# Gates ahead of the attention, squares on GpSimd, and four output tiles begun with four heads, in a Griffin-style decoder layer

## The chip, the cores and the metric

The kernel runs on one core of one Trainium2 chip. The metric is the device time of one execution in microseconds (us); lower is better. Engines are TensorE (PE in the profile; PEld are its weight loads), VectorE (DVE), ScalarE (ACT), GpSimd (POOL) and SyncE (SP), which issues most of the DMAs.

## The reference

One decoder layer on 1024 tokens with 1024 channels, in float32. What matters here is branch A with its gates:

```python
proj = h @ w_in                      # q, k, v, pool input, memory q, gate logits (3 x 1024 columns)
a = diff_attention(q_d, k_d, v_d, lam)        # 8 heads, two softmax maps each, causal, ALiBi
a = rms_norm(a, subln_g) * (1.0 - lam_init)   # per head, over its 128 channels
y_attn = a.reshape(B, S, 1024) @ w_attn_branch
gates = sigmoid(gate_logits).reshape(B, S, 3, 1024)
mix = gates[:, :, 0] * y_attn + gates[:, :, 1] * y_pool + gates[:, :, 2] * y_mem
x = x + rms_norm(mix @ w_out)
```

A gated feed-forward part with a convolution over tokens follows, which the change does not touch.

## The kernel before

**Products.** Every float32 operand is split into a rounded part and the rest (`split`, L87: ScalarE rounds, L89, VectorE subtracts, L90), and a product is three matmuls (`mm3`, L102: high by high, high by low, low by high). Two tiles of 128 output channels over all tokens are either computed directly (`gate`, L1112: 48 matmuls of 128x512 a tile, 96 for two) or together as seven products of half blocks with sums of blocks (`seven`, L198, called by `channels`: 7 x 12 = 84 matmuls for the pair; its weight pages are split just before they are used). Keys' tile pair, the four pairs of queries and gates 0 and 1 go through `seven` ahead of the attention.

**Attention.** Eight heads run in turn, four query blocks of 256 tokens each. A block's stages are `scores` (L1161 on TensorE; L1165 on VectorE adds the bias and takes the maximum, L1170 on ScalarE is the exponential), `combine` (the two maps together, L1181 to L1184 on VectorE), `turn_weights` (transposes, L1200, then a split into aT), `weigh_values` (L1217, the products with the values into poa) and `head_norm` (L1235, the sum of the squares, sq, over the head's channels by two matmuls with ones into pn, stored to ss_d). The squares' high part is rounded on ScalarE (L1225), the low part subtracted on VectorE (L1226). Each block's result goes to DRAM (ao_d). `weave` (L257) puts fillers between the stages: next head's keys, values and queries, and steps of `gate`. The table GATES sets that gate tiles 2 and 3 fill head 0 and tile 4 fills head 7.

**After it.** Gates 5 to 7 run between the last head and the first output product. `load_norms` and `head_norms` turn the sums of four heads into reciprocal norms (hn, small VectorE operations L1260 to L1266) and store them (r_d, L1267); each head is loaded again (a, L1381) with its norm spread over the partitions (rb, L1383), scaled (L1384, VectorE) and split into ath (ScalarE) and atl (VectorE). `merge_heads` (L1356) multiplies heads by the output weights of the branch into pya; output tiles 0 and 1 are begun with heads 0 to 3 while heads 4 to 7 are still on their way. `merge` (L1403) multiplies by the gate and adds the other branches.

**Order.** Each engine runs its instructions in the order of its queue; a scheduler derives it from the code, pools and dependences, and `issue_after` keeps an instruction behind another. DMAs issued on SP's or GpSimd's queue also go in that order.

## Time and profile before

| | before |
|---|---|
| median of 3 runs | 1728.39 us (1727.39 to 1730.04) |
| profiled execution, span | 1727.6 us |
| TensorE | 1712.8 us busy, 8106 matmuls |
| VectorE | 1241.3 us busy |
| ScalarE | 886.6 us busy |
| GpSimd | 45.0 us busy |
| DMA | 294.41 MB, 170 GB/s on average |

The runs are timed without a profile; the profiled execution is one more, and its span runs from the first to the last recorded instruction. Head 0 lies at 605 to 642 us, heads 1 to 7 up to 879 us, and heads 4 to 7 are loaded again at about 903 us. In a timeline's row stand start, duration, engine, line, operation and tiles, then in brackets how long the engine was idle before and what ended that.

### The profile page before, as it was taken

How to read it: one execution, taken by the hardware profiler on the slowest of the kernel's cores; microseconds unless marked ns; L12 is line 12 of the kernel's file. 1: busy time of each engine (PE TensorE's matmuls, PEld its weight loads, DVE VectorE, ACT ScalarE, POOL GpSimd, SP SyncE). 2: the span in 40 equal slices, each digit the busy share in tenths (PEclk: the TensorE clock that was granted, in tenths of full speed). 3: DMA queues.
4: the chain of work that ended last, by engine and by line, in shares of the span. 5: the costliest groups of instructions: out<-in, count | busy, mean ns of one | idle time of the engine just before them, and what ended most of it. 6: DMA issues, size and time to landing. Idle time of an engine off the chain costs nothing.

```text
span 1727.6 us, 22400 instructions
## 1 busy us (share of the span) xinstructions
PE 1712.8 (99%) x8106; PEld 1421.4 (82%) x8106; DVE 1241.3 (72%) x2047; ACT 886.6 (51%) x1577; POOL 45.0 (3%) x103
## 2 busy tenths in 40 slices
PE   9999999999999999999999999999999999999998
PEld 7888888887888888888888888888888888888886
DVE  6765875666665578888866555848888888878466
ACT  5434544434544467777754344645555555543453
POOL 0000000000000011111110000000000000000000
PEclk9999999999999999999999999999999999999999
DMA  8873544444874686665556571572333423583344
GB/s 273 317 281 114 163 150 133 166 147 143 266 237 159 201 231 170 176 182 152 145 187 239 176 230 50 171 225 92 124 112 107 122 85 98 190 299 106 107 149 142
DMA packets 232803, 294.41 MB, mean 170 GB/s; under 512 B 15865, under 2 KB 161526, under 8 KB 230006
## 3 DMA queue, kind: packets, MB, share of 16 engines
q1 hardware_dynamic: 229158, 285.61, 51.8%
q0 software_dynamic: 3520, 7.38, 1.2%
q8 instruction: 64, 1.05, 0.3%
q14 instruction: 45, 0.37, 0.1%
q10 hardware_dynamic: 16, 0.00, 0.0%
HBM read 201.10 MB, written 85.56 MB: 166 GB/s over the span
## 4 chain that ended last, share of the span: by engine, by line
PE 91%; DVE 5%; DMA 2%; ACT 1%; issue 1%; SPq 0%; DVEq 0%; ACTq 0%
PE pa L103 8%; PE pa L104 8%; PE pa L105 8%; PE pb L103 5%; PE pb L104 5%; PE pb L105 5%; PE pss L1161 3%; PE poa L1217 2%; PE pd L103 2%; PE pd L105 2%; PE pd L104 2%; PE pe L105 2%; PE pe L104 2%; PE pe L103 2%; PE pout L103 2%; PE pout L105 2%
## 5 line engine op out<-in xcount | busy, mean ns | idle before, releaser
L89 ACT ACTIVATE wpage<-s 128x512 fp32r<-128x512 f32 x136 | 85.3, 627 | 108.2 <-DVE s L188 35.3
L90 DVE TENSOR_TENSOR wpage<-s,wpage 128x512 fp32r<-128x512 f32 x136 | 92.8, 688 | 43.2 <-ACT wpage L89 43.2
L1565 DVE SCALAR_TENSOR_TENSOR cvt<-gv,cols,cvt 128x1023 f32<-128x1023 f32 x88 | 112.5, 1278 | 15.6 <-ACT cvt L1561 14.9
L1165 DVE CUSTOM_DVE_ANT_0 z<-pss,hbias 128x256 f32<-128x256 f32 (+7 forms) x128 | 94.5, 752 | 26.0 <-PE pss L1161 24.8
L1170 ACT ACTIVATE z<-z,mx 128x256 f32<-128x256 f32 (+7 forms) x128 | 98.8, 773 | 20.8 <-DVE mx L1165 20.7
L103 PE MATMUL pa<-T,wpage 128*128 128x512 f32 x264 | 102.8, 389 | 0.0
L105 PE MATMUL pa<-T,wpage 128*128 128x512 f32 x264 | 102.7, 389 | 0.0
L104 PE MATMUL pa<-T,wpage 128*128 128x512 f32 x264 | 102.7, 389 | 0.0
L1161 PE MATMUL pss<-ks,q 128*128 128x512 f32 (+5 forms) x384 | 86.6, 349 | 1.4 <-DVE mx L1165 1.4
L89 ACT ACTIVATE page<-blk 128x1024 fp32r<-128x1024 f32 (+1 forms) x42 | 41.4, 989 | 85.7 <-PE pe L104 50.6
L90 DVE TENSOR_TENSOR page<-blk,page 128x1024 fp32r<-128x1024 f32 (+1 forms) x42 | 47.5, 1130 | 38.1 <-ACT page L89 38.1
L1161 PEld LDWEIGHTS pss<-ks,q 128*128 128x128 f32 x384 | 62.9, 189 | 11.1 <-DVE mx L1165 6.2
L103 PE MATMUL pd<-page 128*128 128x512 f32 x176 | 68.7, 390 | 0.0
L104 PE MATMUL pd<-page 128*128 128x512 f32 x176 | 68.5, 389 | 0.0
L105 PE MATMUL pd<-page 128*128 128x512 f32 x176 | 68.3, 389 | 0.0
L103 PE MATMUL pa<-hT,wpage 128*128 128x512 f32 x168 | 65.5, 390 | 0.1
L105 PE MATMUL pa<-hT,wpage 128*128 128x512 f32 x168 | 65.4, 389 | 0.0
L104 PE MATMUL pa<-hT,wpage 128*128 128x512 f32 x168 | 65.4, 389 | 0.0
L1217 PEld LDWEIGHTS poa<-aT,v 128*128 128x128 f32 x480 | 60.7, 190 | 3.0 <-ACT srow L1237 1.4
L1217 PE MATMUL poa<-aT,v 128*128 128x256 f32 (+1 forms) x480 | 62.5, 280 | 0.0
L103 PEld LDWEIGHTS pa<-T,wpage 128*128 128x128 f32 x264 | 49.6, 188 | 10.7 <-DVE gv L250 0.3
L104 PEld LDWEIGHTS pa<-T,wpage 128*128 128x128 f32 x264 | 49.6, 188 | 10.2
(429 smaller groups left out, 4965.7 us busy)
## 6 DMA issues: line engine op xcount, KB each, us to landing
q<-q_d SPq DMA_DIRECT2D x64, 256.0 KB, 5.1
wd<-in_w_down_dram SPq DMA_DIRECT2D x22, 512.0 KB, 5.0
tw_d<-wd SPq DMA_DIRECT2D x11, 1024.0 KB
rawv<-in_w_up_dram SPq DMA_DIRECT2D x22, 512.0 KB, 5.8
rawu<-in_w_up_dram SPq DMA_DIRECT2D x22, 512.0 KB, 4.1
ff_d<-cvt SPq DMA_DIRECT2D x22, 512.0 KB, 5.4
blk<-ff_d SPq DMA_DIRECT2D x20, 512.0 KB, 7.9
br<-tw_d SPq DMA_DIRECT2D x20, 512.0 KB, 5.0
```

The lines of the kernel that those rows point to most:

```text
L89: copy = nc.scalar.activation(out=hi, in_=src, func=AF.Copy)
L90: nc.vector.tensor_tensor(out=lo, in0=src, in1=hi.bitcast(F32), op=ALU.subtract)
L103: nc.tensor.matmul(o, ah, bh, start=first, stop=False, skip_group_check=onto)
L104: nc.tensor.matmul(o, ah, bl, start=False, stop=False, skip_group_check=onto)
L105: return nc.tensor.matmul(o, al, bh, start=False, stop=last, skip_group_check=onto)
L1161: last["scores"] = nc.tensor.matmul(pss[:, i * H:i * H + m], q[:, j, c, ts], keys, start=(j == 0), stop=(j == 1))
L1165: nc.vector.tensor_tensor_reduce(out=halves(z[:, 0:n]), in0=pss.rearrange("p (a m) -> p a m", a=2)[:, 0:parts, 0:m], in1=halves(biases[h][ ...
L1170: nc.scalar.activation(out=z[:, 0:n], in_=z[:, 0:n], func=AF.Exp, scale=-1.0, bias=mx[:, c:c + 1], accum_out=sm if c else sums[:, h, t:t + 1])
L1217: nc.tensor.matmul(po[:, qs], (vh, vl)[i][:, k, :], w[j][:, ws], start=(n == 0), stop=(n == len(terms) - 1))
L1565: nc.vector.scalar_tensor_tensor(out=cv[:, sh:], in0=u[:, 0:S - sh], scalar=w, in1=cv[:, sh:], op0=ALU.mult, op1=ALU.add)
```

## The change

It computes gate tiles 2 to 5 as two further pairs through `seven` ahead of the attention, each stored as 1 MB from SP. Gate 6 takes the place of gates 2 and 3 in head 0; gate 7 is split, with four steps in head 7 and four (`tail`) behind the last product with the values. The low part of the squares is subtracted on GpSimd, and the store of ao moves behind it in the code. The pools of the attention are opened in another order. sum_d is stored from ScalarE's queue. The loads of heads 0 to 3 (`load_head`) are issued ahead of the last norms' loads. Output weights are loaded and split in pieces of four heads by two tiles (`merge_weights`), and four output tiles instead of two are begun with heads 0 to 3.

```diff
@@ -1023,22 +1023,26 @@
         for h in range(0, NH, 2):
             split_heads(channels(h * P), q_d[h:h + 2], -0.125)
 
+        for dt in (2, 4):
+            g = channels(C_G + dt * P)
+            nc.sync.dma_start(out=gate_d[dt:dt + 2].rearrange("e p s -> p e s"), in_=g)
+
         ss = gp_.tile([P, 4, H4, P], F32, tag="g", name="ss", bufs=3)
         g01 = [gq.tile([P, S], F32, tag="t", name="g01") for _ in range(2)]
         late = []
         channels(C_G, ss=[ss[:, j] for j in range(4)], g=g01, late=late)
 
-        ready = {2: wsplit(chunk(w_in, C_G + 2 * P), [P, KT, P])}
-        with tc.issue_after(ready[2][2].ins):
+        ready = {6: wsplit(chunk(w_in, C_G + 6 * P), [P, KT, P])}
+        with tc.issue_after(ready[6][2].ins):
             late[0]()
     rstack.close()
     tstack.close()
 
 
     cstack = ExitStack()
+    vpool = cstack.enter_context(tc.tile_pool(name="vp", reuse_waits="tile", bufs=2, side="right"))
+    ap_ = cstack.enter_context(tc.tile_pool(name="att", reuse_waits="tile", bufs=3, side="right"))
     qkp = cstack.enter_context(tc.tile_pool(name="qkp", reuse_waits="tile", bufs=1, side="right"))
-    ap_ = cstack.enter_context(tc.tile_pool(name="att", reuse_waits="tile", bufs=3, side="right"))
-    vpool = cstack.enter_context(tc.tile_pool(name="vp", reuse_waits="tile", bufs=2, side="right"))
 
 
     bias = ap_.tile([P, 1152], F32, name="bias", bufs=1)
@@ -1214,16 +1218,15 @@
         last = (2 * b + 1, slice(P, 2 * P), at[b], slice(2 * P, 3 * P))
         terms[1:1] = [(last, i, j) for i, j in ((0, 0), (0, 1), (1, 0))]
         for n, ((k, qs, w, ws), i, j) in enumerate(terms):
-            nc.tensor.matmul(po[:, qs], (vh, vl)[i][:, k, :], w[j][:, ws], start=(n == 0), stop=(n == len(terms) - 1))
+            ends["poa"] = nc.tensor.matmul(po[:, qs], (vh, vl)[i][:, k, :], w[j][:, ws], start=(n == 0), stop=(n == len(terms) - 1))
         ao = ap_.tile([P, 2 * P], F32, tag="ao", name="ao", bufs=2)
         nc.scalar.activation(out=ao, in_=po, func=AF.Copy)
-        nc.gpsimd.dma_start(out=ao_d[h][:, bs], in_=ao)
-
         sq = ap_.tile([P, 2 * P], F32, tag="sq", name="sq", bufs=1)
         nc.scalar.activation(out=sq, in_=po, func=AF.Square)
         sqs = [ap_.tile([P, 2 * P], F32R, tag="sq%d" % j, name="sq%d" % j, bufs=1) for j in range(2)]
         nc.scalar.activation(out=sqs[0], in_=sq, func=AF.Copy)
-        ends["square"] = nc.vector.tensor_tensor(out=sqs[1], in0=sq, in1=sqs[0].bitcast(F32), op=ALU.subtract)
+        ends["square"] = nc.gpsimd.tensor_tensor(out=sqs[1], in0=sq, in1=sqs[0].bitcast(F32), op=ALU.subtract)
+        nc.gpsimd.dma_start(out=ao_d[h][:, bs], in_=ao)
         pns[h, b] = sqs
         if b == 3:
             vtiles.pop(h)
@@ -1246,13 +1249,14 @@
         nc.tensor.transpose(pt[0:HG * KT, :], sums[:, g * HG:(g + 1) * HG].rearrange("p h t -> p (h t)"), ident)
         row = ap_.tile([HG * KT, P], F32, tag="trow", name="trow", bufs=1)
         nc.scalar.activation(out=row, in_=pt[0:HG * KT, :], func=AF.Copy)
-        nc.sync.dma_start(out=sum_d[g * HG:(g + 1) * HG].rearrange("h (t p) -> (h t) p", p=P), in_=row)
+        nc.scalar.dma_start(out=sum_d[g * HG:(g + 1) * HG].rearrange("h (t p) -> (h t) p", p=P), in_=row)
 
     def load_norms(g):
 
         st = small.tile([P, 4, HG, 8], F32, tag="hn", name="hn", bufs=1)
         for src, r in ((ss_d, 0), (sum_d, 3)):
-            nc.sync.dma_start(out=st[:, r], in_=src[g * HG:(g + 1) * HG].rearrange("h (p f) -> p h f", f=8))
+            with tc.issue_after(marks["head"].ins) if g else nullcontext():
+                nc.sync.dma_start(out=st[:, r], in_=src[g * HG:(g + 1) * HG].rearrange("h (p f) -> p h f", f=8))
         hns[g] = st
 
     def head_norms(g):
@@ -1274,7 +1278,7 @@
     queries(0, 0)
     kts[0] = key_tiles(0)
     load_keys(0)
-    first = gate(2)
+    first = gate(6)
     head_bias(0)
     for _ in range(2):
         next(first)
@@ -1284,10 +1288,8 @@
     load_keys(1)
     last["keys"] = last["load"]
     with tc.issue_after(last["load"].ins):
-        ready[3] = wsplit(chunk(w_in, C_G + 3 * P), [P, KT, P])
         for dt in range(2):
             nc.sync.dma_start(out=gate_d[dt], in_=g01[dt])
-    GATES = ((2, 3), (), (), (), (), (), (), (4,))
     blocks = [(h, b) for h in range(NH) for b in range(4)]
     for h in range(NH):
         stages = []
@@ -1330,19 +1332,29 @@
                 fillers += steps(head_keys(h + 1), 4)
             for n, step in enumerate(steps(values(h + 1), 2)):
                 fillers.insert(2 * n + 1, step)
-        n = 0
-        for dt in GATES[h]:
-            for step in steps(first if dt == 2 else gate(dt), 6 if dt == 2 else 8):
-                fillers.insert(min(n, len(fillers)), step)
-                n += 2
+        if h == 0:
+            for n, step in enumerate(steps(first, 6)):
+                fillers.insert(min(2 * n, len(fillers)), step)
+        if h == NH - 1:
+            tail = steps(gate(7), 8)
+            fillers, tail = fillers + tail[:4], tail[4:]
         weave(stages, fillers)
     combine(*blocks[-1], 1)
     turn_weights(*blocks[-1])
+    mws, pys = {}, {}
+
+    def merge_weights(d, g):
+
+        src = w_attn_branch[g * H:(g + 1) * H, d * 2 * P:(d + 1) * 2 * P]
+        with tc.issue_after(marks["head"].ins if "head" in marks else last["combine"].ins):
+            raw = wload(src.rearrange("(k p) c -> p k c", p=P), [P, H4, 2 * P])
+            mws[d, g] = wsplit(None, [P, H4, 2 * P], raw)[:2]
+
+    merge_weights(0, 0)
     turn_sums(1)
     head_norm(*blocks[-2])
     weigh_values(*blocks[-1])
     head_norm(*blocks[-1])
-    load_norms(1)
     cstack.close()
 
 
@@ -1351,38 +1363,56 @@
     ath = [atp.tile([P, S], F32R, name="ath%d" % h) for h in range(NH)]
     atl = [atp.tile([P, S], F32R, name="atl%d" % h) for h in range(NH)]
 
-    pys = {}
-
-    def merge_heads(dt, g):
+    def merge_heads(d, g):
 
         if g == 0:
-            pys[dt] = wsplit(chunk(w_attn_branch, dt * P), [P, KT, P])[:2] + (bank(name="pya"), pbank(name="pya"))
-        wh, wl, *py = pys[dt]
-        for i in range(2):
-            hs = slice(i * H, (i + 1) * H)
-            for k in range(g * HG, (g + 1) * HG):
-                mm3(py[i], wh[:, k, :], wl[:, k, :], ath[k][:, hs], atl[k][:, hs], k == 0, k == KT - 1)
+            both = ([bank2((P, 2, H), "pya") for _ in range(2)] if d % 2 == 0 else
+                    [(bank(name="pya"), pbank(name="pya")) for _ in range(2)])
+            pys[d] = [[b[:, 0, :], b[:, 1, :]] if d % 2 == 0 else list(b) for b in both]
+        wh, wl = mws.pop((d, g))
+        order = [(k, e, i) for k in range(H4) for e in range(2) for i in range(2)]
+        if d >= 2 and g == 1:
+            order = [(k, e, i) for e in range(2) for i in range(2) for k in range(H4)]
+        for k, e, i in order:
+            h, hs, es = g * HG + k, slice(i * H, (i + 1) * H), slice(e * P, (e + 1) * P)
+            mm3(pys[d][e][i], wh[:, k, es], wl[:, k, es], ath[h][:, hs], atl[h][:, hs], h == 0, h == NH - 1)
 
     with tc.tile_pool(name="sub", reuse_waits="tile", bufs=4, side="right") as sub:
         gs = sub.tile([P, 1], F32, name="gs", bufs=1)
         nc.vector.tensor_scalar(out=gs, in0=cols[:, 1, 44:45], scalar1=1.0 - LAM_INIT, scalar2=None,
                                 op0=ALU.mult)
-        for dt in range(5, KT):
-            for step in steps(gate(dt), 8):
-                step()
-        for h in range(NH):
-            if h == HG:
-                with tc.issue_after(ends["square"].ins):
-                    head_norms(1)
-
-                for dt in range(2):
-                    merge_heads(dt, 0)
+        heads = {}
+
+        def load_head(h):
             a = sub.tile([P, S], F32, tag="a", name="a")
             nc.sync.dma_start(out=a, in_=ao_d[h])
             rb = sub.tile([P, S], F32, tag="rb", name="rb")
-            nc.sync.dma_start(out=rb, in_=r_d[h:h + 1, :].partition_broadcast(P))
+            marks["head"] = nc.sync.dma_start(out=rb, in_=r_d[h:h + 1, :].partition_broadcast(P))
+            heads[h] = a, rb
+
+        def normed_head(h):
+            a, rb = heads.pop(h)
             nc.vector.scalar_tensor_tensor(out=a, in0=a, scalar=gs, in1=rb, op0=ALU.mult, op1=ALU.mult)
             split(ath[h], atl[h], a)
+
+        for h in range(HG):
+            load_head(h)
+        load_norms(1)
+        for n, step in enumerate(tail):
+            with tc.issue_after(ends["poa"].ins) if n else nullcontext():
+                step()
+        for h in range(HG):
+            normed_head(h)
+        merge_weights(1, 0)
+        with tc.issue_after(ends["square"].ins):
+            head_norms(1)
+        merge_heads(0, 0)
+        merge_weights(0, 1)
+        merge_heads(1, 0)
+        merge_weights(1, 1)
+        for h in range(HG, NH):
+            load_head(h)
+            normed_head(h)
     hstack.close()
 
     mstack = ExitStack()
@@ -1402,22 +1432,26 @@
 
     def merge(dt):
 
-        for i, py in enumerate(pys.pop(dt)[2:]):
+        for i, py in enumerate(pys[dt // 2][dt % 2]):
             hs = slice(i * H, (i + 1) * H)
             gm2 = gq.tile([P, 2, H], F32, tag="t", name="gm2")
             g, mp = gm2[:, 0, :], gm2[:, 1, :]
-            nc.sync.dma_start(out=g, in_=gate_d[dt][:, hs])
-            nc.sync.dma_start(out=mp, in_=mixp_d[dt][:, hs])
+            with tc.issue_after(marks["head"].ins):
+                nc.sync.dma_start(out=g, in_=gate_d[dt][:, hs])
+                nc.sync.dma_start(out=mp, in_=mixp_d[dt][:, hs])
             nc.scalar.activation(out=g, in_=g, func=AF.Sigmoid)
             nc.vector.tensor_tensor(out=g, in0=py, in1=g, op=ALU.mult)
             nc.vector.tensor_tensor(out=g, in0=g, in1=mp, op=ALU.add)
             split(mixh[i][:, dt, :], mixl[i][:, dt, :], g)
 
-    for dt in range(KT):
-        if dt >= 2:
-            merge_heads(dt, 0)
-        merge_heads(dt, 1)
-        merge(dt)
+    for d in range(4):
+        if d >= 2:
+            for g in range(2):
+                merge_weights(d, g)
+            merge_heads(d, 0)
+        merge_heads(d, 1)
+        for e in range(2):
+            merge(2 * d + e)
     for k in range(4):
         load_wo(woa, k)
     dstack.close()
```

On TensorE in head 0 the rows are these before; pss2 are scores, pg0 a gate tile's half (hTh, hTl: the layer's normed input), pta turned weights.

```order
L1161 MATMUL pss2_4963<-ks0_4881,q_4876 128x384 x2
L1161 MATMUL pss2_4969<-ks1_4882,q_4876 128x384 x2
L103 MATMUL pg0_4889<-hTh0_110,wh_4849 128x512
L104 MATMUL pg0_4889<-hTl0_112,wh_4849 128x512
L105 MATMUL pg0_4889<-hTh0_110,wl_4850 128x512
L103 MATMUL pg0_4889<-hTh0_110,wh_4849 128x512
L104 MATMUL pg0_4889<-hTl0_112,wh_4849 128x512
L105 MATMUL pg0_4889<-hTh0_110,wl_4850 128x512
L1200 MATMUL pta_4991<-ident_80,z_4927 128x128
L1200 MATMUL pta_4991<-ident_80,z_4941 128x128 x2
```

At the same place now (poa is the block's result):

```order
L1165 MATMUL pss2_5209<-ks0_5135,q_5130 128x384 x2
L1165 MATMUL pss2_5215<-ks1_5136,q_5130 128x384 x2
L1204 MATMUL pta_5228<-ident_80,z_5175 128x128
L1204 MATMUL pta_5228<-ident_80,z_5189 128x128 x2
L1165 MATMUL pss2_5238<-ks0_5135,q_5130 128x512 x2
L1221 MATMUL poa_5253<-aT0_5226,v_5156 128x256
```

The six gate matmuls between the scores and the turned weights are gone.

On ScalarE behind the last product with the values before (wh: a weight's rounded part, trow and srow: sums on their way to DRAM):

```order
L1219 ACTIVATE ao<-poa 128x256
L1223 ACTIVATE sq<-poa 128x256
L1225 ACTIVATE sq_8524<-sq 128x256
L1130 ACTIVATE g_8595<-pg_8570 128x512
L1237 ACTIVATE srow<-pn 1x256
L89 ACTIVATE wh<-raw 128x1024
L1130 ACTIVATE g_8623<-pg_8598 128x512
L89 ACTIVATE ath_8543<-a 128x1024
```

And now:

```order
L1223 ACTIVATE ao<-poa 128x256
L1225 ACTIVATE sq<-poa 128x256
L1227 ACTIVATE sq_8693<-sq 128x256
L1240 ACTIVATE srow<-pn 1x256
L1134 ACTIVATE g_8775<-pg_8750 128x512
L89 ACTIVATE ath_8710<-a 128x1024
L89 ACTIVATE ath_8711<-a 128x1024
L89 ACTIVATE ath_8712<-a 128x1024
L89 ACTIVATE ath_8713<-a 128x1024
```

The eviction of the last gate half now stands directly ahead of the four rounded heads. On TensorE the last matmuls of that half and the first output products (pya) follow each other:

```order
L103 MATMUL pg0_8750<-hTh1_111,wh_8324 128x512
L104 MATMUL pg0_8750<-hTl1_113,wh_8324 128x512
L105 MATMUL pg0_8750<-hTh1_111,wl_8325 128x512
L103 MATMUL pya_8813<-ath0_8710,wh_8649 128x512
L103 MATMUL pya_8814<-ath0_8710,wh_8649 128x512
L104 MATMUL pya_8813<-atl0_8718,wh_8649 128x512
L105 MATMUL pya_8813<-ath0_8710,wl_8650 128x512
```

Eighteen gate matmuls stand between the last product with the values and the first output product, where 125 stood. On VectorE the scaling of heads 0 to 3 (a) and their low halves (atl) now alternate:

```order
L90 TENSOR_TENSOR aT_8640<-pta,aT_8639 128x384
L1382 TENSOR_SCALAR gs<-cols 128x1
L1395 SCALAR_TENSOR_TENSOR a<-a,gs,rb 128x1024
L90 TENSOR_TENSOR atl_8718<-a,ath_8710 128x1024
L1395 SCALAR_TENSOR_TENSOR a<-a,gs,rb 128x1024
L90 TENSOR_TENSOR atl_8719<-a,ath_8711 128x1024
L1395 SCALAR_TENSOR_TENSOR a<-a,gs,rb 128x1024
L90 TENSOR_TENSOR atl_8720<-a,ath_8712 128x1024
```

They follow directly on the last turned weights.

## The prediction

> **What bounds the kernel now.** I read the page's shares and its chain first, then the stretches that the change touches, then the engines' timelines at the end of attention.
>
> ```profile
> span 1727.6 us, 22400 instructions
> PE 1712.8 (99%) x8106; PEld 1421.4 (82%) x8106; DVE 1241.3 (72%) x2047; ACT 886.6 (51%) x1577; POOL 45.0 (3%) x103
> PE 91%; DVE 5%; DMA 2%; ACT 1%; issue 1%; SPq 0%; DVEq 0%; ACTq 0%
> ```
>
> TensorE is busy for 1712.8 of 1727.6 us: only 14.8 us are idle. A change gains by fewer matmuls, or by idle time out of those 14.8; it loses wherever matmuls that lay under a slower chain are taken away. The runs' median, 1728.39, lies 0.8 us above this execution's span, and I add the sum to the median. A measurement of this kernel tells about 0.2% (3.5 us) from no change.
>
> The stretches: the last six pairs of block products, head 0, heads 1 to 7 until shortly before the end, and the last scores to the last product with the values (columns: stretch, its length, then busy time and instructions of PE, PEld, DVE, ACT and POOL, clock, DMA share, GB/s).
>
> ```profile
> 485.00:602.00 117.00, 117.00 (x518) 96.89 (x517) 68.51 (x98) 49.69 (x79) 2.81 (x3) 1.00 0.58 188
> 605.00:642.00 37.00, 36.12 (x199) 30.94 (x198) 26.00 (x66) 23.51 (x56) 4.46 (x8) 1.00 0.81 219
> 648.00:845.50 197.50, 194.37 (x1203) 168.76 (x1202) 170.20 (x448) 149.34 (x367) 25.65 (x48) 1.00 0.63 172
> 866.70:878.90 12.20, 12.20 (x72) 9.69 (x71) 10.26 (x18) 8.68 (x19) 1.61 (x3) 1.00 0.25 76
> ```
>
> In the pairs TensorE never pauses. In the middle heads it pauses for 3.1 us, at full clock, with VectorE busy for 86%.
>
> **The change part by part.**
>
> (1) *Four gate tiles as two pairs.* Four direct tiles are 192 matmuls, two pairs 168.
>
> ```profile
> 602.60 0.39 PE L103 MATMUL pg<-hTh,wh 128*128 128x512 f32 x1
> 605.09 0.39 PE L105 MATMUL pg<-hTh,wl 128*128 128x512 f32 x1
> ```
>
> Eleven steps lie between these starts: 2.49/11 = 0.2265 us each. The pairs keep that pace (117.00 us for 518 matmuls, 0.226), with VectorE busy for 59%, so their operand work (14 pages a pair) and 1 MB stores lie beside TensorE. 24 × 0.2265 = 5.4: **−5.4**.
>
> (2) *Keys of head 0.* The second half of the keys is loaded once the third-last product is out of PSUM; behind it stand 24 gate matmuls, and 12 more of other work, before the first scores: 36 × 0.2265 = 8.2 us.
>
> ```profile
> DMA to landing us min/median/max: 7.8/9.6/9.8
> ```
>
> That is the keys' loads around head 0, issue to landing. Against 8.2 the bounds are 0 and 1.6; the loads behind which these wait are the two halves of one head, as in the row: I take **+0.5**.
>
> (3) *Head 0.* Of its 96 gate matmuls 48 go: 10.9 us. TensorE then needs 37.0 − 10.9 = 26.1 us.
>
> ```profile
> L90 DVE TENSOR_TENSOR aT<-pta,aT 128x384 fp32r<-128x384 f32 (+1 forms) x6 | 3.5, 619 | 1.3 <-ACT aT L89 1.3
> L1181 DVE RECIPROCAL mx<-sm 128x1 f32<-128x1 f32 x8 | 1.3, 163 | 5.0 <-ACT z L1170 4.9
> L1226 DVE TENSOR_TENSOR sq<-sq,sq 128x256 fp32r<-128x256 f32 x3 | 1.3, 421 | 1.3 <-ACT sq L1225 1.3
> L90 DVE TENSOR_TENSOR wl<-raw,wh 128x1024 fp32r<-128x1024 f32 x1 | 1.2, 1219 | 0.0
> ```
>
> These are VectorE's groups in that stretch (busy, mean ns | idle before it). VectorE's 26.0 lose 1.3 (squares) and 1.2 (one weight): 23.5. Its waits for ScalarE, 5.0 (the reciprocal for its exponential) and 1.3 (the turned weights), belong to the block's own chain and stay: 29.8 in all, 3.7 above TensorE's 26.1. Bounds 0 (the waits overlap other blocks) and 3.7; nearer the upper, as no filler is left to part the blocks: **+2.8**.
>
> (4) *Squares in heads 1 to 6.* VectorE is relieved of 24 × 0.42 = 10.1 us, but TensorE was idle only 3.1 there (197.50 − 194.37), which bounds the gain; part of it belongs to the start of a head. Between 0 and −3.1: **−1.5**. That a square is ready later on GpSimd costs nothing here: the sum that reads it stands a block behind, some 8 us (197.5/24); the cover is gone after the last block alone (6).
>
> (5) *Head 7.* Of 66 gate matmuls ahead of the last product with the values 30 remain: 18 before the last scores (36 in the kernel before) and 12 behind them (30).
>
> ```profile
> 866.90 1.22 DVE L1165 CUSTOM_DVE_ANT_0 z<-pss,hbias 128x1024 f32<-128x1024 f32 x1 [0.26 <-PE pss L1161]
> 868.05 1.15 DVE L90 TENSOR_TENSOR aT<-pta,aT 128x512 fp32r<-128x512 f32 x2
> 873.38 1.23 DVE L90 TENSOR_TENSOR wl<-raw,wh 128x1024 fp32r<-128x1024 f32 x1
> 874.53 0.42 DVE L1226 TENSOR_TENSOR sq<-sq,sq 128x256 fp32r<-128x256 f32 x1
> 878.93 3.00 PE L1217 MATMUL poa<-aT,v 128*128 128x256 f32 x24
> ```
>
> ```profile
> PE pss L1161 <- DVE mx L1165: 1.4, 4, 0.5
> PE pta L1200 <- DVE z L1184: 1.3, 3, 0.6
> ```
>
> In the first part, 18 × 0.2265 = 4.1 us of cover go while VectorE loses little. TensorE's waits for VectorE in the whole attention (total, times, longest) have been 0.5 and 0.6 us at most, so one to three of them are the bounds: 0 to 1.5, **+0.5**. From the last scores to that product VectorE's chain takes 12.2 us (866.7 to 878.93). Afterwards it lacks the square (0.42) and one turned weight (0.58); a weight's low half (1.23) still stands in it: 11.2. TensorE's work there falls from 12.2 by 18 × 0.2265 = 4.1 to 8.1. The gap is 3.1; bounds 2 (if the weight's half comes later) and 4: **+3.0**.
>
> (6) *Last square.* TensorE's second sum of squares now waits for GpSimd.
>
> ```profile
> 882.65 0.42 ACT L1225 ACTIVATE sq<-sq 128x256 fp32r<-128x256 f32 x1
> 882.64 0.56 POOL L1220 DMA_DIRECT2D ao_d<-ao  x1 [2.35 <-ACT sq L1223]
> 883.59 0.39 PE L1235 MATMUL pn<-sq,ones 128*128 128x256 f32 x1
> L1047 POOL TENSOR_SCALAR_AFFINE_SELECT bias<-bias 128x1152 f32<-128x1152 f32 x1 | 1.6, 1612 | 0.0
> masks.py:199 POOL TENSOR_SCALAR_AFFINE_SELECT ident<-ident 128x128 f32<-128x128 f32 x1 | 0.3, 288 | 0.0
> ```
>
> No row shows this operation on GpSimd. Its own elementwise rows bound it: 0.29 us for 128 columns, 1.61 for 1152; on the line between, 256 columns are 0.45 (an estimate from these two). In program order it stands behind the issue that ends at 883.20, so ends at 883.65 where the matmul started at 883.59; bounds 0.1 and 1.5, **+0.4** with the semaphore's way. [...]
>
> (7) *Heads 0 to 3 into the output tiles.* Before, 125 gate matmuls (28 us) stood between the last product with the values and the first output matmul; now 18. ScalarE evicts gate 7 (g) ahead of the first rounded head (ath), and g waits for TensorE's last gate matmul.
>
> ```profile
> 882.92 0.39 PE L105 MATMUL pg<-hTh,wl 128*128 128x512 f32 x1
> 883.35 0.60 ACT L1130 ACTIVATE g<-pg 128x512 f32<-128x512 f32 x1 [0.28 <-PE pg L105]
> 894.96 1.06 ACT L89 ACTIVATE ath<-a 128x1024 fp32r<-128x1024 f32 x1 [4.39 <-DVE a L1384]
> 893.64 1.28 DVE L1384 SCALAR_TENSOR_TENSOR a<-a,gs,rb 128x1024 f32<-128x1024 f32 x1 [0.40 <-DMA rb<-r_d]
> 896.05 1.23 DVE L90 TENSOR_TENSOR atl<-a,ath 128x1024 fp32r<-128x1024 f32 x1 [0.57 <-ACT ath L89]
> 897.20 1.28 DVE L1384 SCALAR_TENSOR_TENSOR a<-a,gs,rb 128x1024 f32<-128x1024 f32 x1
> ```
>
> Eviction starts 0.04 after the matmul's end (883.31 to 883.35). From that matmul's start: 0.39 + 0.04 + 0.60 + 1.06 + 0.04 = 2.13 until ath may be used; the next matmul could have started after 0.23, so TensorE stands for 1.9. Two matmuls (0.45) go before the low half (atl, 1.23) is wanted: 0.8 more with 0.04. VectorE's order is then scale, atl, scale, atl, so a head takes 3.56 us (893.64 to 897.20: scale 1.28, ScalarE's ath, atl) where its 12 matmuls take 2.72: 3 × 0.83 = 2.5. Together **+5.2**; bounds 4.5 and 6. The scaling of head 0 is early, since its loads were moved ahead on SP.
>
> (8) *Heads 4 to 7.* From the fourth head's atl: a weight's half, ten small norm operations, the store of the norms, their loads, the next scaling and ath.
>
> ```profile
> 893.04 0.19 DVE L152 TENSOR_TENSOR hn<-hn 128x32 f32<-128x32 f32 x1
> 895.51 0.37 SPq L1267 DMA_DIRECT2D r_d<-hn  x1
> 903.49 0.33 SPq L1383 DMA_DIRECT2D rb<-r_d  x1
> 908.92 1.28 DVE L1384 SCALAR_TENSOR_TENSOR a<-a,gs,rb 128x1024 f32<-128x1024 f32 x1 [2.05 <-DMA rb<-r_d]
> sum_d<-trow SPq DMA_DIRECT2D x2, 16.0 KB, 2.4
> ```
>
> The store took 8.0 us before (895.51 to 903.49, when rb may be issued), behind 512 KB loads; the store of the same size in the last row takes 2.4. SP's queue now holds the loads of heads 4 to 6, which were issued earlier; I take 2.4. So 1.2 + 10 × 0.23 (the pace of the rows around 893.04) + 0.1 + 2.4 + 5.4 (903.49 to 908.92) + 1.28 + 1.06 = 13.7 us. TensorE has 56 matmuls there (10 of head 3 and 46 of the second pair): 12.7. Thus 1.0, and then atl of head 4 behind a second scaling: 1.28 + 1.23 − 1.06 − 3 × 0.2265 = 0.8, and of head 5 behind a scaling and a weight: 3.74 − 15 × 0.2265 = 0.4. **+2.2**; bounds 0.8 and 7.8 (8.0 in place of 2.4).
>
> GpSimd's move of the issue behind the square, sum_d's store on ScalarE's queue and the changed pool order I cost at nothing: what is queued behind the square on GpSimd are stores of heads, norms and gates that are read back a head later or more, and GpSimd is busy for 3%; sum_d is read by the norm loads of (8), ahead of which the sums of the last squares must land anyway.
>
> Sum: −5.4 + 0.5 + 2.8 − 1.5 + 0.5 + 3.0 + 0.4 + 5.2 + 2.2 = **+7.7**, or 1728.4 + 7.7 = 1736.1.
>
> **The rivals.**
>
> *The norms' store lands late* (8.0 us again): +5.6, 1741.7. For it: heads' loads of 512 KB stand ahead on the same queue. Against: they wait for atl of heads 0 to 2, and can be done.
>
> *GpSimd's square holds VectorE up*, so that the relief of (4) is nothing: 7.7 + 1.5 = 9.2, 1737.6. No row of this trace has both engines on elementwise work together. [...]
>
> *No change that can be measured*: ScalarE's waits overlap in (3) (−2.8), head 7 loses 2 (−1.0), the middle heads give all 3.1 (−1.6): +2.3, 1730.7. For it: every one of these is at a bound that rows allow.
>
> *Faster*: the middle heads run at VectorE's pace, TensorE's records hiding its pauses. For it: VectorE has 5% of the chain (86 us), where TensorE's waits name it with 1.4 and 1.3 us. A square then costs up to its 0.42 and its wait for ScalarE (1.3/3 = 0.43 in head 0): 24 × 0.85 = 20.4 in place of 1.5: 7.7 + 1.5 − 20.4 = −11.2, 1717.2. It breaks even at 9.2/24 = 0.38 a square, and is faster by over 3.5 from 0.53. Against: 3.1 us of idle time in 197.5.
>
> **How the numbers follow.** My forecast, lost cover, 0.54; the late store 0.10; GpSimd's hold 0.04; no change 0.20; faster 0.12. Slower is 0.54 + 0.10 + 0.04 = 0.68. The range reaches from 1728.5, which leaves out the faster case and the lower part of no change, to 1743, past the late store. The forecast's own range is 1732 to 1741.
>
> **What would show it.** A stop of TensorE of about 2 us between gate 7's last matmul and the first output matmul, ended by ScalarE's ath, and some 0.8 us before each atl (7); stops of some 3 us before the last product with the values (5); about 1 us at head 4's ath, ended by the loads of r_d (8); TensorE's idle time up from 14.8 to about 28 (13.1 more: 7.7 + 5.4); GpSimd's square near 0.45 us. It is wrong if the middle heads shrink by much more than 3 us, or if ath of head 0 is done before TensorE's last gate matmul.

## The result and the profile after

The changed kernel takes 1745.84 us (median of 4 runs, 1745.35 to 1746.30) against 1728.27 for the kernel before (four runs by then): a ratio of 1.0101, interval 1.0087 to 1.0116, or 17.6 us slower. The forecast was 7.7 slower, in a range that ended at 1743. The profiled execution is one of those four; it took 1745.62 us, 1.7 more than its span.

The head of the page:

```profile
span 1743.9 us, 22400 instructions
PE 1717.1 (98%) x8082; PEld 1418.1 (81%) x8082; DVE 1246.2 (71%) x2039; ACT 890.7 (51%) x1587; POOL 65.9 (4%) x127
```

TensorE has 24 matmuls fewer, yet is busy for 4.3 us more, and idle for 26.8 us in place of 14.8. Busy time that grows while work falls says that matmuls have become slower somewhere, so the granted clock is to be read as well: it is 0.996 on average, where 0.999 stood before.

The stages, cut at the same instructions in both traces (first scores of heads 0, 2 and 7; first output product; first matmul with w_out; the end), in us:

| kernel | to first scores | heads 0, 1 | heads 2 to 6 | head 7 to first output product | output products | from w_out to the end |
|---|---|---|---|---|---|---|
| before | 605.32 | 68.78 | 163.78 | 72.93 | 87.04 | 729.75 |
| after | 640.85 | 62.32 | 164.93 | 46.72 | 91.32 | 737.76 |
| matmuls fewer, by 0.2265 | -38.05 | 10.87 | 0 | 32.62 | 0 | 0 |
| lost | -2.5 | 4.4 | 1.2 | 6.4 | 4.3 | 8.0 |

The last row is the difference of the two, less what the matmuls explain. The first column's -2.5 is no gain of the change: the three kernels that start like the kernel before (itself among them) reach their first scores between 602.9 and 605.3 us, and ten with two pairs between 640.8 and 643.4. The averages, 603.9 and 641.8, differ by 37.9, the price of the two pairs.

The largest loss lies where the change touches nothing, at the first matmuls with w_out. TensorE's longest waits after the change (total, times, longest):

```profile
PE pout L103 <- ACT woh L89: 2.8, 1, 2.8
PE pss L1165 <- DVE mx L1169: 2.5, 8, 0.5
PE pta L1204 <- DVE z L1188: 2.0, 8, 0.4
PE pya L103 <- ACT ath L89: 1.6, 1, 1.6
PE pta L1204 <- DVE aT L90: 1.6, 2, 1.4
...
PE pout L104 <- DVE wol L90: 1.2, 1, 1.2
```

Here wol and woh are the low and the rounded half of w_out, and pout its product. In ScalarE's timeline the rounding (woh) stands behind the sigmoids (L1442) of the last gates:

```profile
998.22 0.61 ACT L1442 ACTIVATE gm<-gm 128x512 f32<-128x512 f32 x1
1004.07 0.63 ACT L1442 ACTIVATE gm<-gm 128x512 f32<-128x512 f32 x1 [5.24 <-issue]
1010.32 0.63 ACT L1442 ACTIVATE gm<-gm 128x512 f32<-128x512 f32 x1 [2.38 <-DMA gm<-gate_d]
1012.97 0.61 ACT L1442 ACTIVATE gm<-gm 128x512 f32<-128x512 f32 x1
1013.49 1.99 ACT L89 ACTIVATE woh<-rawo 128x1024 fp32r<-128x1024 f32 x2
```

The weights themselves were on SP's queue at 1000.53; what is late are the gates, which SP issued at 1005.97 and 1008.69, when a merge had given its buffer back. SP's own waits between 1000 and 1010 us are all for the subtraction that ends a merge (mixl):

```profile
1000.53 0.90 SPq L1428 DMA_DIRECT2D rawo<-in_w_out_dram  x2
1005.97 0.33 SPq L1440 DMA_DIRECT2D gm<-gate_d  x1
1008.69 0.32 SPq L1440 DMA_DIRECT2D gm<-gate_d  x1
```

```profile
SPq L1440 <- DVE mixl L90: 8.7, 3, 4.4
```

From the gate's issue at 1005.97 to its sigmoid at 1010.32 another 4.4 us pass, and the roundings of w_out stand behind it.

And TensorE there (windows; the column behind POOL is the clock):

```profile
1006.10:1011.70 5.60, 5.60 (x25) 4.32 (x24) 2.52 (x4) 1.26 (x2) 0.00 (x0) 1.00 0.68 241
1011.70:1016.90 5.20, 1.13 (x3) 0.69 (x3) 4.46 (x7) 4.46 (x7) 0.00 (x0) 0.88 0.62 197
1016.90:1022.50 5.60, 5.60 (x15) 4.35 (x14) 4.65 (x5) 2.15 (x4) 0.00 (x0) 0.50 0.91 264
```

TensorE stands for about 4 us and then works at half clock: 15 matmuls in 5.6 us where 25 went before. Measured at equal matmuls, the gap to the kernel before grows by 4.9 us over the two stops and has reached 7.5 when full clock returns, nearly the whole 8.0 of this stage.

Why the merges are late is seen at their beginning, in VectorE's product of an output piece with its gate. Before:

```profile
924.61 0.69 DVE L1412 TENSOR_TENSOR gm<-pya,gm 128x512 f32<-128x512 f32 x1 [1.25 <-PE pya L105]
```

After:

```profile
951.48 1.29 DVE L1443 TENSOR_TENSOR gm<-pya,gm 128x512 f32<-128x512 f32 x2 [2.06 <-PE pya L105]
```

The first output product starts at 910.8 and 914.8 us. So the first piece is finished 14 us later before, and 37 us later after, since four tiles are begun together and none is complete until heads 4 to 7 arrive. The same 16 merges then have 55 us until the products end, 3.4 each; from 951.5 to 1013.7 they ran at 4.1 each.

### The profile page after: what moved, and what is told of

Read it like the earlier page. It is cut to its first block, busy times and chain, and to the rows that moved or that the text cites. A ratio compares the mean times of both kernels' runs of the same rounds, so it can differ in the third digit from the quotient of the medians.

```text
span 1743.9 us, 22400 instructions
## 1 busy us (share of the span) xinstructions
PE 1717.1 (98%) x8082; PEld 1418.1 (81%) x8082; DVE 1246.2 (71%) x2039; ACT 890.7 (51%) x1587; POOL 65.9 (4%) x127
## 5 line engine op out<-in xcount | busy, mean ns | idle before, releaser
L89 ACT ACTIVATE wpage<-s 128x512 fp32r<-128x512 f32 x144 | 90.3, 627 | 115.1 <-DVE s L188 49.4
L90 DVE TENSOR_TENSOR wpage<-s,wpage 128x512 fp32r<-128x512 f32 x144 | 98.1, 687 | 48.8 <-ACT wpage L89 48.8
L103 PE MATMUL pa<-hT,wpage 128*128 128x512 f32 x192 | 74.7, 389 | 0.0
L104 PE MATMUL pa<-hT,wpage 128*128 128x512 f32 x192 | 74.7, 389 | 0.0
L105 PE MATMUL pa<-hT,wpage 128*128 128x512 f32 x192 | 74.7, 389 | 0.0
```

The lines of the kernel that those rows point to most:

```text
L89: copy = nc.scalar.activation(out=hi, in_=src, func=AF.Copy)
L90: nc.vector.tensor_tensor(out=lo, in0=src, in1=hi.bitcast(F32), op=ALU.subtract)
L103: nc.tensor.matmul(o, ah, bh, start=first, stop=False, skip_group_check=onto)
L104: nc.tensor.matmul(o, ah, bl, start=False, stop=False, skip_group_check=onto)
L105: return nc.tensor.matmul(o, al, bh, start=False, stop=last, skip_group_check=onto)
```

## The experiments

**The last tiles one after the other.** Tiles 4 to 7 get all eight heads and are merged singly:

```diff
-            merge_heads(d, 0)
-        merge_heads(d, 1)
-        for e in range(2):
-            merge(2 * d + e)
+            for e in range(2):
+                merge_heads(d, 0, (e,))
+                merge_heads(d, 1, (e,))
+                merge(2 * d + e)
```

> The changed kernel, with output tiles 4 to 7 computed and merged one after the other again (all eight heads of a tile, then its merge) instead of two tiles together; everything else of the change stays. Theory A: the stop of 4.4 us behind the 24th matmul with w_out and the slow clock after it (8.0 us in all from the first such matmul to the end) come from four finished pieces that follow each other 2.7 us apart, while the gates for them have two buffers and ScalarE holds the rounding of w_out behind their sigmoids: the stop goes, about 1738 us (-7 to -9). Rival B: gate loads are late because of SP's queue behind the weights' pieces, whatever the order of the products: the stop stays, 1745 to 1747. Rival C: the stop goes but the work it waited for shows up later in the stage: 1741 to 1744.

1745.43 us (1.0102, 1.0088 to 1.0116): no gain, theory A fell, and rival B's time came out, though its reason (SP's queue behind the weights) was not tested by it. TensorE's waits at w_out:

```profile
PE pout L104 <- DVE wol L90: 1.7, 1, 1.7
PE pout L103 <- ACT woh L89: 1.2, 1, 1.2
```

The stop is 2.9 in place of 4.1 us, and still there, with the last gates again issued late (1004.54 and 1009.30 us). The profiled execution also shows how a small shift costs time elsewhere. The same stops at the end of head 7, in this kernel and in the changed one:

```profile
900.00:904.00 4.00, 1.96 (x13) 1.30 (x13) 3.22 (x4) 2.06 (x4) 0.47 (x1) 1.00 0.66 251
904.00:908.00 4.00, 3.37 (x15) 3.18 (x16) 2.03 (x4) 0.64 (x2) 0.51 (x1) 0.56 0.02 4
```

```profile
900.00:904.00 4.00, 1.68 (x13) 1.03 (x11) 3.22 (x5) 2.06 (x4) 0.15 (x1) 1.00 0.64 249
904.00:908.00 4.00, 3.64 (x28) 3.42 (x29) 1.71 (x3) 0.67 (x3) 0.51 (x1) 1.00 0.02 4
```

In the first kernel half clock follows from 904.5 to 911.3, in the changed one it does not: 49.3 against 46.7 us from head 7 to the first output product.

**The squares back on VectorE**, all else as in the change:

```diff
-        ends["square"] = nc.gpsimd.tensor_tensor(out=sqs[1], ...)
+        ends["square"] = nc.vector.tensor_tensor(out=sqs[1], ...)
```

> The changed kernel with the low half of the squares subtracted on VectorE again (32 instructions of 0.42 us instead of 32 of 0.76 on GpSimd). Theory A: TensorE bounds the middle heads, so the squares' place is worth nothing there, and the two waits of TensorE for GpSimd's square (0.7 us) go: 1744.5 to 1746. Rival B: GpSimd's instruction holds VectorE up (its scaling of the maps went from 827 to 878 ns): 1742 to 1744. Rival C: the relief was real and covered other losses: 1747 to 1750.

1744.14 us, 1.7 below the change: in rival B's range, though the intervals of the two (1.0080 to 1.0107 and 1.0087 to 1.0116) overlap. In the profile heads 2 to 6 are 1.6 us shorter. Other stages move as well, both ways: head 7 is 2.5 longer, with half clock from 902.9, and the stage from w_out is 732.7 in place of 737.8, with the same two buffers. Why, no run shows; the stop at w_out differs much from profile to profile. **The squares alone on GpSimd**, in the kernel before (the same line the other way):

> The kernel before with nothing changed but the low half of the squares on GpSimd. Theory A: TensorE bounds the heads and the last square is covered by gate matmuls: 1727.5 to 1729 (no change). Rival B: GpSimd's hold of VectorE costs time: 1729.5 to 1732. Rival C: relief of VectorE: 1725 to 1727.

1730.35 us against 1728.03 (1.0013, 1.0004 to 1.0022): 2.3 us slower, rival B again. Heads 2 to 6 take 163.3 to 163.4 us in the five other kernels in which VectorE has the squares and head 0 has half its gates, 163.8 before, and 164.9 to 165.2 in the seven with the squares on GpSimd. VectorE's scaling of the maps in heads 2 to 6, for the width of 768 columns before and in this kernel:

```profile
L1184 DVE SCALAR_TENSOR_TENSOR z<-z,mx 128x768 f32<-128x768 f32 x5 | 5.1, 1012 | 0.0
```

```profile
L1184 DVE SCALAR_TENSOR_TENSOR z<-z,mx 128x768 f32<-128x768 f32 x5 | 7.5, 1498 | 0.0
```

The seven other widths stayed within 4 ns: it is the scaling of 768 columns alone that meets a square on GpSimd, once a head. Such a meeting in this kernel (first two rows), and one the other way round in the changed kernel (last two):

```profile
696.88 0.73 POOL L1226 TENSOR_TENSOR sq<-sq,sq 128x256 fp32r<-128x256 f32 x1 [0.81 <-ACT sq L1225]
696.92 1.50 DVE L1184 SCALAR_TENSOR_TENSOR z<-z,mx 128x768 f32<-128x768 f32 x1
898.28 1.28 DVE L1188 SCALAR_TENSOR_TENSOR z<-z,mx 128x1024 f32<-128x1024 f32 x1
898.82 1.33 POOL L1228 TENSOR_TENSOR sq<-sq,sq 128x256 fp32r<-128x256 f32 x1
```

In both pairs of rows the one that starts second takes longer. VectorE's scaling, both operands in SBUF, starts 0.04 us behind GpSimd and takes 1.50 us in place of 1.01, five times 0.49 in this stage; GpSimd's square takes 1.33 us, where the median is 0.74, when VectorE's scaling has begun before it. VectorE's subtraction with one operand in PSUM (ktmp) kept its 0.69 us beside a square.

**The pairs alone**, with gates 6 and 7 placed as in the change, and the squares, loads and merges of the kernel before:

```diff
+        for dt in (2, 4):
+            g = channels(C_G + dt * P)
+            nc.sync.dma_start(out=gate_d[dt:dt + 2]..., in_=g)
...
-        for dt in range(5, KT):
-            for step in steps(gate(dt), 8):
-                step()
+        for step in tail:
+            step()
```

> The kernel before with gates 2 to 5 as two pairs ahead of the attention, gate 6 in head 0 and gate 7 half in head 7 and half behind the last product with the values; squares on VectorE, two output tiles begun with four heads and one tile after the other as in the kernel before. Theory A (cover): 24 matmuls fewer (-5.4), some 4 lost in heads 0 and 1, some 4 in head 7, and behind the attention a longer stop than in the changed kernel, since 48 + 48 matmuls less cover heads 4 to 7: 10 to 18 us slower than before, 1738 to 1746, with the stop before the first output products of head 4 and none at w_out. Rival B (the loss lies in the new merges and GpSimd): 1724 to 1731.

1751.60 us (1.0137, 1.0123 to 1.0151), worse than the whole change and than theory A's 1746. One wait says why:

```profile
PE pya L103 <- ACT ath L89: 14.0, 2, 13.8
```

Without the early loads of heads 0 to 3, the first output product waits 13.8 us, with half clock in and behind the wait (913.6 to 930.7 us). With two tiles begun and merged as before no wait for w_out's halves shows, and the gap there grows by 0.6 us in place of 7.5, though the buffers are the same two: the stop there comes with the new merges. The other parts of the change thus bring back some 6 us of a loss that the pairs make.

**One gate out of head 0**, in the kernel before. This kernel leaves gate 3 out (gate 2 is stored in its place):

```diff
-    GATES = ((2, 3), (), (), (), (), (), (), (4,))
+    GATES = ((2,), (), (), (), (), (), (), (4,))
```

> The kernel before without gate 3 in head 0: 48 matmuls less (10.9 us by their pace), a copy of gate 2 stands in for it. Step 3 of the prediction: if the gates in head 0 are the cover of a chain over ScalarE and VectorE, the time falls by 6 to 8 us (1720 to 1722) and heads 0 and 1 by the same. Rival: TensorE bounds head 0 with one gate as well: it falls by 10.9, to 1717.

1721.98 us against 1728.22: 6.2 less for 10.9 us of matmuls. Heads 0 and 1:

```profile
602.89:665.31 62.42, 59.34 (x347) 49.79 (x346) 51.66 (x135) 45.92 (x111) 8.70 (x16) 1.00 0.77 216
```

62.42 us as in the changed kernel (62.32), with neither pairs nor GpSimd's squares: the gates in head 0 were cover for 4.5 us.

**Four buffers for the merges.**

```diff
+    gmp = dstack.enter_context(tc.tile_pool(name="gmp", reuse_waits="tile", bufs=2, side="right"))
...
-            gm2 = gq.tile([P, 2, H], F32, tag="t", name="gm2")
+            gm2 = (gmp if dt % 2 else gq).tile([P, 2, H], F32, tag="t", name="gm2")
```

> The changed kernel with four instead of two buffers for the merges' gates and other branches (tiles of odd number take theirs from a pool of their own); nothing else. New theory D: begun four at a time, no output tile is finished until 37 us after the first output product (14 in the kernel before), and the 16 merges that are left then run at the pace of two buffers, 4.1 us each (load, sigmoid, product, sum, split), while TensorE's products for one take 3.4: the merges end 10 us behind the products and hold the rounding of w_out up. With four buffers the merges are no longer the bound: the stops at w_out (4.9 us) and the half clock behind them (2.4 us) go: 1737.5 to 1739. Rival E: it is not the buffers but ScalarE's and SP's order, or the loads' time, that keeps the merges back: 1743 to 1746.

1743.26 us, 2.6 below the change, which had run on another chip. Both again, side by side on one chip:

> The changed kernel again, so that the next two can be held against it on one chip: 1744 to 1747.

> The changed kernel with four buffers for the merges, once more, beside the changed kernel itself. The profiled execution of the first try lost the stop at w_out (that stage 6.7 us shorter), while its times lay only 2.6 us below those of the changed kernel on another chip. Theory D (backlog of merges): 5 to 8 us below the changed kernel of this chip. Rival: what is gained there is lost to half-clock stretches elsewhere: 1 to 4 us below.

1745.91 us for the change and 1743.47 with four buffers. In the profiles the stage from w_out to the end falls from 737.8 and 736.6 us to 731.0 and 732.4 (729.8 before). Of the waits there this is left, in the first and in the second profile with four buffers:

```profile
PE pout L104 <- DVE wol L90: 0.6, 1, 0.6
```

```profile
PE pout L104 <- DVE wol L90: 0.8, 1, 0.8
PE pout L103 <- ACT woh L89: 0.2, 1, 0.2
```

So the backlog makes the stop: theory D holds for the stage, 4 to 7 us. All five profiles with four buffers end this stage in 730.2 to 732.5 us, the five with two buffers and the new merges in 732.7 to 737.8. In the times only 2.4 arrive, as the rival of the second try had it, and by the times alone rival E (1743 to 1746) could not be told apart. One part of the reason is which executions were profiled: the first profile with four buffers is the fastest of its four runs (1741.32), the change's second the slowest (1747.69). Another is shown: in the second profile the stage ahead of it is 2.3 us longer than in the change's (48.99 against 46.73) with half clock after 903, which the change's did not have. For the rest of the difference there is no profile.

**Buffers, and squares back.**

> As with four buffers for the merges, and the squares' low half on VectorE again. If the two losses are separate (squares on GpSimd 1.7 to 2.3 us): 1735.5 to 1737.5. If the second hides behind the first: as with four buffers alone.

1740.11 us, 3.2 below four buffers alone: the two losses are separate. The range for that, 1735.5 to 1737.5, was missed all the same, because four buffers alone had gained less than it counted on. **And two heads ahead of gate 7's eviction:**

```diff
+            if n == len(tail) - 2:
+                normed_head(0)
+                normed_head(1)
...
-            nc.scalar.activation(out=g, in_=pg, func=AF.Copy)
+            with tc.issue_after(marks["ath"].ins) if "ath" in marks else nullcontext():
+                nc.scalar.activation(out=g, in_=pg, func=AF.Copy)
```

> As the last one (four buffers, squares on VectorE), and the first two heads are scaled and rounded on ScalarE ahead of the eviction of gate 7's last half, instead of behind it. Step 7 of the prediction: TensorE's stop of 1.6 to 1.8 us before the first output product goes, and with it the half clock behind it (some 2 us for 4 us): 2 to 4 us faster than the last one, 1732 to 1735. Rival: the chain of VectorE (scale, low half, scale, low half) takes over at once, and the heads behind wait as long: 0 to 1 us faster.

1738.89 us (1736.31 to 1743.14): 1.2 less, too little to tell from nothing. The 1.6 us wait for the first head went, and others came, in the waits of the output products:

```profile
PE pya L104 <- DVE atl L90: 1.4, 3, 0.8
PE pya L103 <- ACT ath L89: 1.3, 1, 1.3
```

The first is VectorE's chain, as the rival said; the second is head 4.

**The stop filled with useless matmuls**, eight behind gate 7:

```diff
+            if dt == KT - 1 and i:
+                with tc.issue_after(last["gate"].ins):
+                    pf = pbank(name="pfill")
+                    for n in range(8):
+                        nc.tensor.matmul(pf, wh[:, 0, :], hTh[1][:, 0, :], start=(n == 0), stop=(n == 7))
```

> The changed kernel with eight useless matmuls of 128x512 (into a PSUM tile that nobody reads) between gate 7's last matmul and the first output product, where TensorE stands for 1.6 to 1.8 us. Theory: the half clock of TensorE that follows such stretches (4.8 us from 916 us on) comes from too little work in a stretch of some 4 us and costs about 2 us: with the stop filled it goes, and the kernel gets no slower, or 1 to 2 us faster, although it does 1.8 us more work. Rival: the half clock comes from the stops before (901 to 905 us) or at random: the same time or up to 1 us slower, with the half clock still there.

1746.96 us, 1.1 above the change beside it. It settles nothing: half clock came earlier in this profile, from 904.9 to 911.7 us, as in some kernels without the filling, and none came behind the filled place.

**One pair only**: gates 4 and 5 in head 0, gate 6 in head 7, gate 7 behind it, with four buffers, squares on VectorE and four heads rounded ahead of the last eviction.

> Gates 2 and 3 alone as a pair ahead of the attention; gates 4 and 5 fill head 0 and gate 6 fills head 7 as in the kernel before, gate 7 stands wholly behind head 7, its last eviction behind the four rounded heads; four output tiles begun with four heads as in the changed kernel, four buffers for the merges, squares on VectorE. If the losses were the cover taken out of heads 0 and 7 and from behind the attention, the merges' backlog and GpSimd's squares, then what is left is 12 matmuls fewer (-2.7) and stops of 0 to 1.5 us: 1725 to 1727.5. Rival: four tiles begun together cost time by themselves, or 42 gate matmuls behind the last product with the values do not cover the heads' chains: 1729 to 1734.

1732.37 us (1.0025, 1.0016 to 1.0035). Heads 0 and 1 (69.1 us) and 2 to 6 (163.7) are back at the level of the kernel before, and the end of the attention has half clock no more. But from head 7 to the first output product 54.2 us stand where 72.9 less 96 matmuls gives 51.2: 3.0 lost, with 1.3 in the output products and 1.4 behind; 1732.37 lies in the rival's range. The longest waits in the attention:

```profile
PE pta L1205 <- DVE z L1189: 1.8, 4, 0.6
PE pg L105 <- DVE wl L90: 1.5, 2, 1.3
```

Of these, 0.6 and 1.3 us come between 891 and 894 us, and 0.9 and 0.4 for the sums behind them: the 3.0. The two tiles of one pair, too, are missed as cover at the end of the attention, and 12 matmuls (2.7 us) do not pay for that. Whether the four tiles begun together cost something besides was not separated.

## Why the prediction was wrong, by its steps

- **The direction and TensorE's idle time were right.** Idle time rose to 26.8 us, where about 28 stood in the prediction. That agreement is partly luck, since the 4 us at w_out were not in it.
- **(1) and (2)** held: the pairs cost 37.9 us for 168 matmuls (38.05), and the keys' loads cost nothing that shows, at the lower bound.
- **(3)** was right in kind and too small: 4.4 us lost in heads 0 and 1 where +2.8 stood, less a share of (4). Leaving a gate out gives 4.5 by itself.
- **(4) had the wrong sign.** 1.5 us of relief were forecast; on GpSimd the squares cost 1.2 in heads 2 to 6 (1.6 against the kernels with 163.3), and 2.3 in all when moved alone: the square holds up VectorE's scaling (1.50 us in place of 1.01), and TensorE has no use for the relief. The 3.1 us of idle TensorE were rightly read as a ceiling for the gain, but GpSimd's hold of VectorE, a rival at 0.04 that was priced as no gain and not as a loss, is what happened. That no row of the trace before had both engines on elementwise work was not quite so: GpSimd's 1.61 us row lies beside a VectorE subtraction with both operands in SBUF, which kept its 0.69 us. That subtraction had started first (593.07 against 593.16 us), so these rows show no VectorE instruction that starts second. What was 0.45 us by the line through two GpSimd rows with one operand was 0.74 to 0.77.
- **(5), (6) and the first stop of (7)** held: 6.4 us lost from head 7 to the first output product, where 0.5, 3.0, 0.4 and 1.9 stood. The stop ahead of the output product was named with its releaser:

```profile
912.80 0.39 PE L105 MATMUL pg<-hTh,wl 128*128 128x512 f32 x1
914.82 0.73 PE L103 MATMUL pya<-ath,wh 128*128 128x512 f32 x2 [1.63 <-ACT ath L89]
916.08 0.50 PE L104 MATMUL pya<-atl,wh 128*128 128x512 f32 x1 [0.53 <-DVE atl L90]
```

- **The rest of (7), and (8)**: 4.3 us against 5.5, with the mechanism only in part as told. In this profile half clock follows the first stop (916.7 to 920.1 us), and TensorE, with 0.43 us from matmul to matmul there and so some 5.1 for a head's 12, is then slow enough for VectorE's chain of heads (3.5 and 3.6 us from one atl to the next). Where the clock stayed full, the stops before atl were 0.5 to 0.9 us, as told. The norms' store was not late:

```profile
930.34 0.37 SPq L1271 DMA_DIRECT2D r_d<-hn  x1
932.13 1.76 SPq L1390 DMA_DIRECT2D rb<-r_d  x4
```

1.8 us in place of 2.4 (8.0 in the rival), and two of the three loads of heads issued ahead of it had landed, at 926.20 and 927.45; for the third the trace shows no landing.

- **The step that failed is a term that was not there.** The prediction followed cover taken away up to heads 4 to 7 and stopped. It took four tiles begun together as cover alone, and did not ask when the first of them would be finished, and what then has to pass two buffers. In the profile that is 8.0 us where nothing stood, most of the 8.7 by which the losses of the table (21.8) exceed those of the sum (13.1); in the second profile of the same kernel the stage lost 6.8. A sign of it stood in the trace before: the first merge came 14 us behind the first output product, and the last sigmoid waited 3.9 us for its gate even there:

```profile
997.41 0.63 ACT L1411 ACTIVATE gm<-gm 128x512 f32<-128x512 f32 x1 [3.89 <-DMA gm<-gate_d]
```

- **In the times of whole kernels that step and (4) weigh alike.** Four buffers gave back 2.4 us with the squares on GpSimd and 4.0 with them on VectorE; the squares back on VectorE gave 1.7 with two buffers and 3.2 with four (the 1.7 and the 4.0 are not for certain from one chip). Both together are 5.8 us (1745.91 to 1740.11, one chip). With the 1.5 that (4) had counted as a gain that makes 7.3 of the 10.0 that the forecast missed there. The remaining 2.7 are spread: (3) was 1.6 too small, and for the rest no run singles a cause out.

- **A second kind of cost had no term:** half clock. The prediction counted each stop by its length. At w_out about 2.6 of the 7.5 us were half clock.

## What to carry to other kernels

Work that fills TensorE is cover: before moving it, look up in the trace which chain it hides, and price the move by that chain, not by the matmuls saved. Where more results are begun at once, ask when the first one is finished, and whether their consumers keep up from there with the buffers that they have. And moving an elementwise instruction to an idle engine is not free: here it stood in the way of the very engine that it was to relieve, which took 1.50 us for an instruction of 1.01. Judge a stage by more than one profile, too: this one's loss at w_out was 8.0 us in one execution and 6.8 in another of the same kernel.

## What was not expected of the hardware

TensorE's clock fell to one half behind stretches that were only partly idle. The largest single wait ahead of it was 1.6 us in the changed kernel (half clock from 916.70 us) and 1.4 in the kernel with single last tiles (from 904.47). In the first profile with four buffers it came within head 1 (from 672.84), where no wait was over 0.5 us.

The clock records of the traces have a regular pattern. Away from a kernel's end each half-clock stretch lasts 3.413 us, twice that, or, over the long wait of the pairs alone, five times that (913.6 to 930.7). In the changed kernel it is once from 916.70 and twice from 1015.69. Two stretches of one execution begin a whole number of 3.413 us apart: 29.0 of them between 916.70 and 1015.69 in the changed kernel, 72.0 between 672.84 and 918.60 with four buffers. So half clock begins and ends on a grid of 3.413 us in these records.

How this grid lies against the work may decide whether half clock comes: that is my reading of two executions, and no run tests it. Here is the place in head 1, cut at each execution's own grid, with four buffers and in the changed kernel:

```profile
669.42:672.84 3.42, 2.05 (x14) 1.38 (x13) 2.72 (x12) 3.42 (x11) 1.27 (x2) 1.00 0.94 354
672.84:676.25 3.41, 3.31 (x12) 2.55 (x12) 2.77 (x8) 2.05 (x7) 0.00 (x0) 0.50 0.52 209
```

```profile
667.52:670.94 3.42, 2.58 (x18) 1.90 (x17) 2.33 (x9) 3.42 (x12) 1.35 (x3) 1.00 0.98 318
670.94:674.35 3.41, 2.52 (x12) 1.51 (x13) 3.32 (x11) 2.55 (x8) 0.03 (x1) 1.00 0.69 279
```

TensorE was busy for 60% of the one window (2.05 of 3.42 us) and half clock followed; the windows of the changed kernel divide the same work otherwise, 75 and 74%, and it did not. Counted so in all traces, the window ahead of each of the 15 drops away from the kernels' ends was busy for 15 to 60%, and no window at full clock without a drop behind it, the first and last 30 us left out, was busy for less than 52%. In the changed kernel it was 40% ahead of 916.70 (1.36 of 3.41 us) and 15% ahead of 1015.69 (0.50 of 3.42), and 59% (2.01 of 3.42, from 899.63) in the least busy one without a drop behind it. Half clock followed at 60%, then, and not at 59 or 52: the busy share alone does not settle it in these traces.

In the changed kernel's profile the half clock behind the stop at w_out costs about 2.6 us. Whether kernels with such stops also scatter more from run to run is not shown: one of them lay between 1736.3 and 1743.1, but the changed kernel's first four runs within 1 us.
